# The AB layer's gaps: unread products ahead of the first weights, x by a second queue, gate rows in three pieces, an earlier reload of x

## The chip, the cores and the metric

One core of a Trainium2 chip runs the whole program. The metric is the device time of one execution in microseconds, the median over several runs. TensorE multiplies, VectorE and ScalarE work on tiles, GpSimd (POOL) does some elementwise work, and SyncE (SP) issues most transfers; ScalarE can issue transfers too. Each engine runs its own instructions strictly in order. The profile also gives the share of full clock speed that TensorE was granted.

## The reference

The program is one step of a small decoder trunk on 544 rows (a prompt of 512 and 8 samples of 4), in float32. Layer 0 is the AB mixer (four mLSTM heads and four GLA heads out of one input projection, one output projection) and an MLP; layer 1 is an SSD mixer and an MLP. After each of the four blocks comes a residual sum and a layernorm.

```
mq, mk, mv, mo, mi, mf, gq, gk, gv, gg, ga = split(x @ w_in)
ml  = headnorm(mLSTM(mq, mk, mv, gates(mi, mf))) * sigmoid(mo)
gla = headnorm(GLA(gq, gk, gv, decay(ga))) * silu(gg)
x   = LN(alpha * x + concat(ml, gla) @ w_out)
x   = LN(alpha * x + squared_relu(x @ w1) @ w2)
```

The states of both mixers, for the prompt and for the samples, are outputs as well.

## The kernel before

Activations lie with features on the 128 partitions and rows along the free axis, in two halves of 272 rows. To keep float32 accuracy each dense product is split: a weight tile `whi` + `wlo` and an activation `xh` + `xl`, and `dense` issues three products (hi hi, hi lo, lo hi) for each of eight blocks of features, so 24 for a tile and a half. `WeightStream` loads a weight tile (`wraw`, three buffers), ScalarE casts it to `whi` and VectorE subtracts to get `wlo`. `take_x` does the same with x; the gate's weight tile (the first) and the first half of x come in four pieces each, piece by piece in turn, all by SyncE's queue.

TensorE's order is the order in which the code is written. Beside the dense products run lanes: generators (`gla_lane`, `ml_lane`, `tokmajor`) that are advanced by `tick()`, which `dense` calls ahead of each product. A lane that yields a number n stays still for n products, so the table `W` spaces the small work (W["gates"] = 120 is the distance from the gates' rows to their use). `need(key)` makes a lane wait until a key is ready. The other engines' instructions are put in order by a scheduler's estimate, except where `hold()` keeps some behind named instructions.

The dense tiles of the AB layer are the gate, gq, gk, gv, mq, mk, mv, gg and mo (25 tiles in all, five at the start for one half of the rows after the other, four at the end likewise). The names that matter here:

- `head_out` makes one head's output: products `num` into two PSUM tiles, statistics on VectorE, `hf` and `hn` (the normalised head) on ScalarE with `hb` from VectorE, then, one step later, the transposes `hot` and the scaled result `cg`.
- `ml_gates` computes the gates' rows: cumulative sums and maxima on 4 partitions in the tiles `rw` and `uw`, after all GLA scores; then, 120 products later, TensorE's transposes `uwt` and eight small products `sc`.
- `ml_head` is one mLSTM head: `row_bc` copies a row to all partitions (`rowbc`), VectorE and ScalarE make the decay matrix `E` of it, GpSimd masks it, products `md`, `mo1`, `mo2` give the scores, and `head_out` ends it. `pipeline` runs the steps of several heads together; the tuple (3, 0, 1, 2) says which step of which head comes first.
- `sample` handles the eight samples' state; its 32 small products are `snum`.
- `finish` multiplies with the output gate and splits into xh and xl; then the residual of the output projection reads x again (`xf`, reloaded by `load_xf` on ScalarE's queue) when a PSUM tile of it is evacuated.

PSUM tiles for dense products are `psd` (three). All others come from `pm`:

```
k = spare[0] and turn[0] % 5 == 0
return psm.tile([P, 512], F32, tag="k" if k else "m", name=name, bufs=1 if k else 4)
```

so four calls in five rotate over four banks and each fifth call gets a fifth bank. SBUF tiles of the AB layer lie in one pool, `ab`; the pool of xf is opened when that is closed.

Of the kernel before, what the change touches and what calls it, by code (L numbers as in the profile page):

```python
# [34 lines left out]
W = dict(dec=12, gates=120, sc=16, lev=14, v=8, kd=10, out=38, ss=40, end=12, c0=20, u=13, s=16, ml=12, mr=40, dt=238, sg=72, sx=14, sq=26, so=48, l0=12, l1=12, v0=64, v1=55, f0=16, f1=18)  # L35
# [192 lines left out]
def trunk_kernel(ctx, tc, a, stages=("ab", "mlp0", "ssd", "mlp1")):  # L228
# [15 lines left out]
    S.preload_act_table_set("natural_log_exp_and_others")  # L244

# [41 lines left out]
    def take_x(pool, bufs=12):  # L287

        loaded = [None]

        def part(h, k):
            t = pool.tile([P, 2, TH], F32, tag="ft", name="xin", bufs=bufs)
            loaded[0] = nc.sync.dma_start(out=t, in_=a["xT"][h, :, k:k + 2]).ins
            split(xh[h][:, k:k + 2], xl[h][:, k:k + 2], t)
        order = {mybir.EngineType.SP, mybir.EngineType.Activation, mybir.EngineType.DVE}
        with tc.high_priority(), tc.manual_schedule(engines=order):
            ws._emit([lambda k=k: part(0, k) for k in range(0, KT, 2)])
            ws.ahead(HEAD)
            for k in range(0, KT, 2):
                part(1, k)  # L300
        nc.sync.dma_start(out=lnp, in_=a["lnp"])
        return loaded[0]
# [322 lines left out]
    def ab(pool):  # L625
# [13 lines left out]
        selr = pool.tile([P, 4, P], F32R, name="selr", bufs=1)  # L639
# [16 lines left out]
        rb = pool.tile([P, NP], F32R, name="rb", bufs=1)  # L656
# [82 lines left out]
        def head_out(mx, key, h, sT, enm=None):  # L739
# [33 lines left out]
            V.scalar_tensor_tensor(nb, mean, -1.0, f, ALU.mult, ALU.mult)  # L773
            hn = sc("hn")
            for i in range(4):
                S.activation(hn[:, i * P:(i + 1) * P], num[i][:, :128], AF.Identity, scale=f[:, i:i + 1], bias=nb[:, i:i + 1])
# [148 lines left out]
        def gla_scores():  # L925
# [7 lines left out]
            for j in range(2):  # L933
                z = pool.tile([P, NP], F32, name=f"zk{j}", bufs=1)
                G.memset(z, 0.0)
                zk.append(z)
            skz = gla["skz"] = [pool.tile([P, 2, 4, NS], F32, name=f"skz{j}", bufs=1) for j in range(2)]
# [3 lines left out]
            for q in range(2):  # L941
                sT = gla["sT"][q] = pool.tile([P, 10, 2, P], F32, tag="sT", name="sT", bufs=2)
# [12 lines left out]
                for L in LEVELS[::-1] + (128, 256):  # L955
# [12 lines left out]
                    zq = pool.tile([P, 2, 256], F32, tag="zq", name="zq", bufs=2)  # L968
# [37 lines left out]
        def hold():  # L1006

            st = ExitStack()
            for x in gla["last"]:
# [83 lines left out]
        def ml_gates():  # L1093
            rw = pool.tile([P, T], F32, name="rw", bufs=1)
            uw = pool.tile([P, T], F32, name="uw", bufs=1)
# [4 lines left out]
            yield from need("gscores")  # L1100
            with hold():
# [11 lines left out]
                V.tensor_tensor_scan(out=M, data0=M, data1=u1, initial=0.0, op0=ALU.add, op1=ALU.max)  # L1113
# [845 lines left out]
```

## Time and profile before

| | us |
|---|---|
| median of three runs (lowest to highest) | 1535.07 (1534.1 to 1536.0) |
| the profiled execution | 1528.88 |
| its span | 1527.2 |
| TensorE busy / VectorE / ScalarE / GpSimd | 1485.8 / 1091.9 / 794.9 / 235.8 |
| first product of the first layernorm (the AB mixer is over) | 288.30 |

The profile is of one execution. "Busy" of TensorE counts a product from its start to its modelled end, and products overlap, so a busy TensorE need not be at its best rate; the granted clock and the time from product to product say more. In a row of the timeline stand the start, the length, the engine, the line of the kernel, the operation, output <- inputs, shapes, and in brackets how long the engine was idle ahead of it and whom it waited for.

### The profile page before, as it was taken

The page shows a single profiled execution, that of the slowest core. Times are in us where ns is not written, and L with a number is a line of the kernel's source. Part 1 is how long each engine was busy: PE and PEld are TensorE (multiplying, and loading weights), DVE is VectorE, ACT ScalarE, POOL GpSimd, SP SyncE. Part 2 cuts the span into 40 slices and gives each one's busy share as a digit, 9 for nine tenths or more (in the row PEclk, how much of TensorE's full clock was granted, in tenths as well). Part 3 has the DMA queues.
Part 4 walks back from the last instruction along what each step waited for, and adds up shares of the span by engine and source line. Part 5 has one row for each costly group of instructions (what it writes and reads, how often), then busy time and mean ns, then how long its engine had stood idle before and what let it go on. Part 6 is the DMA issues. An engine that isn't in the chain of part 4 may idle for free.

```text
span 1527.2 us, 29115 instructions
## 1 busy us (share of the span) xinstructions
PE 1485.8 (97%) x11611; PEld 1434.4 (94%) x11611; DVE 1091.9 (72%) x2004; ACT 794.9 (52%) x1727; POOL 235.8 (15%) x298
## 2 busy tenths in 40 slices
PE   8999999999999999999999999999999999999997
PEld 7999999899999999999888788989999999999996
DVE  4974476676776677667899988777678677676656
ACT  5644447374444444536786675554347345345343
POOL 0510322010000000022454444420020000000000
PEclk9999999999999999999999999999999999999998
DMA  6321213403333232425457767364222332333221
GB/s 218 96 69 42 101 46 97 174 23 107 99 99 97 84 97 83 142 76 176 118 132 251 228 188 237 97 195 152 72 73 70 94 90 92 97 91 91 69 84 59
DMA packets 81200, 172.10 MB, mean 113 GB/s; under 512 B 9240, under 2 KB 35736, under 8 KB 80808
## 3 DMA queue, kind: packets, MB, share of 16 engines
q1 hardware_dynamic: 52248, 141.20, 29.7%
q10 hardware_dynamic: 26032, 18.29, 4.5%
q0 software_dynamic: 2784, 10.75, 1.8%
q8 instruction: 91, 1.49, 0.4%
q14 instruction: 45, 0.37, 0.1%
HBM read 153.48 MB, written 16.73 MB: 111 GB/s over the span
## 4 chain that ended last, share of the span: by engine, by line
PE 80%; DVE 10%; ACT 4%; DMA 3%; issue 2%; SPq 0%; POOL 0%; ACTq 0%; DVEq 0%
PE psd L361 53%; PE psd L504 17%; DVE wlo L167 2%; ACT whi L166 1%; PE num L749 1%; DVE acc L1442 1%; DMA h0n<-h0n 1%; PE yp L1548 1%; ACT xf L440 1%; PE gs L979 1%; PE it L1595 1%; DVE h0n L1608 1%; PE sp L1526 1%; DMA wraw<-mlp_w 1%; PE ip L1523 1%
## 5 line engine op out<-in xcount | busy, mean ns | idle before, releaser
L361 PE MATMUL psd<-xh,whi 128*128 128x272 f32 x1504 | 447.9, 298 | 9.7 <-ACT xh L283 5.0
L361 PE MATMUL psd<-xh,wlo 128*128 128x272 f32 x1504 | 444.7, 296 | 0.4 <-DVE wlo L167 0.4
L361 PE MATMUL psd<-xl,whi 128*128 128x272 f32 x1504 | 442.2, 294 | 2.5 <-DVE xl L284 2.5
L361 PEld LDWEIGHTS psd<-xh,whi 128*128 128x128 f32 x1504 | 287.1, 191 | 16.8 <-issue 7.7
L361 PE MATMUL psd<-hh,whi 128*128 128x272 f32 x1024 | 296.6, 290 | 4.1 <-DVE xf L395 3.0
L361 PEld LDWEIGHTS psd<-xl,whi 128*128 128x128 f32 x1504 | 287.4, 191 | 9.7 <-DVE xl L284 4.3
L361 PE MATMUL psd<-hh,wlo 128*128 128x272 f32 x1024 | 295.7, 289 | 0.0
L361 PE MATMUL psd<-hlo,whi 128*128 128x272 f32 x1024 | 295.4, 288 | 0.2
L361 PEld LDWEIGHTS psd<-xh,wlo 128*128 128x128 f32 x1504 | 287.0, 191 | 4.4 <-issue 2.6
L167 DVE TENSOR_TENSOR wlo<-wraw,whi 128x1024 fp32r<-128x1024 f32 (+2 forms) x173 | 208.2, 1206 | 65.3 <-ACT whi L166 63.5
L166 ACT CAST whi<-wraw 128x1024 fp32r<-128x1024 f32 (+2 forms) x173 | 174.2, 1011 | 152.3 <-PE psd L361 134.0
L361 PEld LDWEIGHTS psd<-hh,whi 128*128 128x128 f32 x1024 | 192.8, 188 | 6.3 <-DVE xf L395 4.9
L361 PEld LDWEIGHTS psd<-hlo,whi 128*128 128x128 f32 x1024 | 192.8, 188 | 0.7 <-DVE hlo L284 0.6
L361 PEld LDWEIGHTS psd<-hh,wlo 128*128 128x128 f32 x1024 | 192.8, 188 | 0.2
L395 DVE TENSOR_TENSOR xf<-xf,psd 128x272 f32<-128x272 f32 x208 | 88.4, 435 | 77.9 <-PE psd L361 77.4
L504 PE MATMUL psd<-xh,whi 128*128 128x272 f32 x416 | 120.2, 289 | 1.0 <-DVE xf L395 1.0
L504 PE MATMUL psd<-xh,wlo 128*128 128x272 f32 x416 | 119.9, 288 | 0.0
L504 PE MATMUL psd<-xl,whi 128*128 128x272 f32 x416 | 119.6, 288 | 0.0
L202 ACT CAST whi<-wsum 128x1024 fp32r<-128x1024 f32 x52 | 54.3, 1044 | 120.4 <-PE psd L504 72.0
L202 ACT CAST whi<-wraw 128x512 fp32r<-128x512 f32 (+1 forms) x52 | 43.2, 835 | 97.4 <-PE psd L361 83.8
L203 DVE TENSOR_TENSOR wlo<-wsum,whi 128x1024 fp32r<-128x1024 f32 x52 | 63.7, 1225 | 23.1 <-ACT whi L202 23.1
L504 PEld LDWEIGHTS psd<-xh,whi 128*128 128x128 f32 x416 | 78.2, 188 | 1.7 <-DVE xf L395 1.5
(475 smaller groups left out, 2824.5 us busy)
## 6 DMA issues: line engine op xcount, KB each, us to landing
wraw<-mlp_w SPq DMA_DIRECT2D x80, 512.0 KB, 3.7
wraw<-ssd_in SPq DMA_DIRECT2D x40, 512.0 KB, 4.2
wraw<-mlp_w SPq DMA_DIRECT2D x64, 256.0 KB, 3.1
wraw<-ab_in SPq DMA_DIRECT2D x24, 512.0 KB, 3.7
h<-h SPq DMA_DIRECT2D x32, 256.0 KB, 4.3
h0n<-h0n SPq DMA_DIRECT2D x16, 512.0 KB, 4.9
E<-d_cs ACTq DMA_DIRECT2D x16, 512.0 KB, 4.7
s_h<-h0n POOLq DMA_DIRECT2D x16, 512.0 KB, 4.7
```

The costliest lines, as they stand in the source:

```text
L166: nc.scalar.copy(hi[:, r], w[:, r])
L167: nc.vector.tensor_tensor(lo[:, r], w[:, r], hi[:, r].bitcast(F32), ALU.subtract)
L202: self.cut[0] = nc.scalar.copy(hi, x).ins
L203: self.cut[1] = nc.vector.tensor_tensor(lo, x, hi.bitcast(F32), ALU.subtract).ins
L361: last[0] = TE.matmul(ps[:, :TH], wt[:, k, :], rt, start=i == 0, stop=i == n - 1).ins
L395: V.tensor_tensor(x, x, ps, ALU.add)
L440: S.activation(x[:, j], x[:, j], AF.Identity, scale=g[:, j:j + 1], bias=b[:, j:j + 1])
L504: last[0] = TE.matmul(ps, wt[:, k], bt[:, k], start=first and n == 0, stop=n == 11, skip_group_check=not first).ins
L749: TE.matmul(num[i], sT[:, i] if j == i else sT[:, (4, 7, 9)[j] + i - j - 1], vt[key][:, j, h, :w], start=j == 0, stop=j == i)
L979: TE.matmul(p[:, 2 * m * b:2 * m * (b + 1)].rearrange("p (e t) -> p e t", e=2), z[:, 2 * m * b:2 * m * b + P], zq[:, :, m * b:m * (b + 1)] ...
L1442: V.scalar_tensor_tensor(acc[:, :n], ci[:, w:w + n], cw[:, m, w:w + 1], acc[:, :n], ALU.mult, ALU.add)
L1523: TE.matmul(ip[:, j * P:(j + 1) * P], hT[:, j * P:(j + 1) * P], Cf[:, tk], start=True, stop=True)
```

## The change

1. `take_x`: the four pieces of the first half of x are loaded by ScalarE's queue ahead of everything else on it; the activation table is loaded after that (it was ScalarE's first instruction).
2. `warm`, a new lane, issues products of `ones` with `ones` into a PSUM tile that nobody reads: nine ahead of the first dense product, two after each of the first three groups of six, and four more after the gate tile. It takes a turn of `pm`, so all later turns move by one.
3. `ml_gates` waits for the first, second and third GLA head in place of the end of the scores, and its three pieces are held behind the last instructions (`hb`, `hn`) of those heads. `uwt` comes 30 products after the fourth head, and `sc` in two parts, 8 products apart.
4. The order of steps in the mLSTM pipeline becomes (3, 1, 2, 0): the row copy of the newest head comes last.
5. Some tiles of the AB layer move to a second pool, `early`, on the right side of SBUF. It is closed after the first half of the last four tiles (`then()`), and the pool of xf opens there, so xf's four loads are written at that place.

```diff
-W = dict(dec=12, gates=120, sc=16, ...
+W = dict(dec=12, gates=30, gr=8, sc=16, ...
-    S.preload_act_table_set("natural_log_exp_and_others")
...
+        def load(eng, h, k):
             t = pool.tile([P, 2, TH], F32, tag="ft", name="xin", bufs=bufs)
-            loaded[0] = nc.sync.dma_start(out=t, in_=a["xT"][h, :, k:k + 2]).ins
+            return t, eng.dma_start(out=t, in_=a["xT"][h, :, k:k + 2]).ins
+
+        def cut(h, k, t):
             split(xh[h][:, k:k + 2], xl[h][:, k:k + 2], t)
...
-            ws._emit([lambda k=k: part(0, k) for k in range(0, KT, 2)])
+            ts = [load(S, 0, k)[0] for k in range(0, KT, 2)]
+            S.preload_act_table_set("natural_log_exp_and_others")
+            ws._emit([lambda k=k: cut(0, 2 * k, ts[k]) for k in range(KT // 2)])
...
+            mx["head"] = [v.ins, s.ins]
+            ready.add((key, h))
             yield
...
-            yield from need("gscores")
-            with hold():
+            yield from need(("g", 0))
+            with hold("head"):
                 S.activation(t, z, AF.Abs)
...
+            yield from need(("g", 1))
+            with hold("head"):
                 m = b
...
+            yield from need(("g", 2))
+            with hold("head"):
                 nM = uw[96:100]
...
+            yield from need(("g", 3))
             yield W["gates"]
             p = pm("uwt")
...
+            yield W["gr"]
             p = pm("sc")
...
+            yield W["gr"]
             for q in range(2):
...
-            yield from pipeline([ml_head(h) for h in range(4)], W["mr"], (3, 0, 1, 2))
+            yield from pipeline([ml_head(h) for h in range(4)], W["mr"], (3, 1, 2, 0))
...
+        def warm():
+            w = pm("warm")
+            for n, gap in ((9, 6), (2, 5), (2, 5), (2, 5), (4, None)):
+                for _ in range(n):
+                    TE.matmul(w[:, :P], ones, ones, start=True, stop=True)
+                if gap:
+                    yield gap
+
+        launch(warm(), "warm")
...
                 until("mheads")
+                then()
...
+                def take_place():
+                    early.close()
+                    xs.append(stk.enter_context(tc.tile_pool(name=f"x{n}", bufs=1, side="right", reuse_waits="tile")))
+                    new_xf(xs[0])
+                    for h in range(2):
+                        for k in range(0, KT, 4):
+                            load_xf(h, k)
```

The tiles `selr`, `rb`, `zk`, `skz`, `sT`, `zq`, `rw`, `uw` and the mLSTM heads' `E` are those that move to `early`.

What stands on SyncE's queue at the start, before and after. `wraw<-ab_gate` are the gate tile's pieces, `xin<-xT` pieces of x, `wraw<-ab_in` whole weight tiles; the counters DMAHW0 to 7 are taken in turn by all transfers in the order of the program, and a wait for one is a wait for an earlier transfer's landing. Before:

```order
L162 DMA wraw<-ab_gate 128x256
L293 DMA xin<-xT 128x544
L301 DMA lnp<-lnp 128x64
L162 DMA wraw<-ab_gate 128x256
L645 DMA prm<-ab_prm 128x13
L293 DMA xin<-xT 128x544
L162 DMA wraw<-ab_gate 128x256 [waits DMAHW0_49]
L293 DMA xin<-xT 128x544 [waits DMAHW1_49]
L165 DMA wraw<-ab_in 128x1024 [waits DMAHW2_49]
L165 DMA wraw<-ab_in 128x1024 [waits DMAHW3_49]
```

After (x's first half is on ScalarE's queue, with the counters 0, 2, 4 and 6):

```order
L162 DMA wraw<-ab_gate 128x256 x3
L302 DMA lnp<-lnp 128x64
L647 DMA prm<-ab_prm 128x13 [waits DMAHW0_49]
L162 DMA wraw<-ab_gate 128x256 [waits DMAHW1_49]
L165 DMA wraw<-ab_in 128x1024 [waits DMAHW2_49]
L165 DMA wraw<-ab_in 128x1024 [waits DMAHW3_49]
```

The last gate piece now stands behind a wait for the first piece of x, and the first whole weight tile waits for the second piece of x.

TensorE's order where the third mLSTM head's row is copied (`psd` rows are dense products). Before:

```order
L361 MATMUL psd<-xh_73,whi 128x272
L676 MATMUL rowbc<-rb,selr 128x256 x2
L1188 MATMUL md<-mq,kz 128x128 x4
L1191 MATMUL mo_2165<-mq,kz 128x384
L1194 MATMUL mo_2168<-mq,kz 128x256
L1195 MATMUL mo_2168<-mq,kz 128x128
L749 MATMUL num<-vt,E 128x130 x10
L361 MATMUL psd<-xl_75,whi 128x272
```

After:

```order
L362 MATMUL psd<-xh_72,whi 128x272
L1199 MATMUL md<-mq,kz 128x128 x4
L1202 MATMUL mo_2173<-mq,kz 128x384
L1205 MATMUL mo_2176<-mq,kz 128x256
L1206 MATMUL mo_2176<-mq,kz 128x128
L751 MATMUL num<-vt,E 128x130 x10
L678 MATMUL rowbc<-rb,selr 128x256 x2
L362 MATMUL psd<-xl_74,whi 128x272
```

The row copy went from the front of the step to its end; the rest stayed.

ScalarE's order where xf is loaded. Before, behind the casts of three weight tiles of the output projection:

```order
L283 CAST xh_74<-sy 128x4x32
L283 CAST xh_74<-cg 128x240
L166 CAST whi<-wraw 128x1024 x3
L310 DMA xf_3062<-xT 128x1088 x2
L310 DMA xf_3063<-xT 128x1088 x2
L166 CAST whi<-wraw 128x1024 x2
```

After, in the first of the last four tiles (`mo`), between the third and the last mLSTM head's normalisation (`hn`, `hf`):

```order
L778 ACTIVATE hn<-num,hb,hf 128x128 x4
L726 ACTIVATE mo<-psd 128x272
L727 ACTIVATE mo<-mo 128x272
L728 ACTIVATE mo<-mo 128x272
L730 ACTIVATE mo<-mo 128x272
L311 DMA xf_2852<-xT 128x1088 x2
L311 DMA xf_2853<-xT 128x1088 x2
L772 ACTIVATE hf<-hf,epsc 128x4
L773 ACTIVATE hf<-hf 128x4
```

The four loads moved ahead by some forty of ScalarE's instructions.

51 lines of the change are left out of this document (25 added, 26 removed).

## Prediction, made before the changed kernel ran

> **What bounds the kernel now.** I read the page's first part, then the waits of TensorE over the AB layer (0 to 420 us of the span), then its busy time and granted clock in slices of 2 us, and last the timeline around each place found.
>
> ```profile
> span 1527.2 us, 29115 instructions
> ...
> PE 1485.8 (97%) x11611; PEld 1434.4 (94%) x11611; DVE 1091.9 (72%) x2004; ACT 794.9 (52%) x1727; POOL 235.8 (15%) x298
> ```
>
> TensorE is busy for 1485.8 of 1527.2 us, so only 41 us of it are idle in the whole span, and what the change can win is idle time or slow time of TensorE. These are its waits in the AB layer (engine, what it ran, whom it waited for, us in total, times, longest):
>
> ```profile
> engine line waited for: us in total, times, longest us
> PE psd L361 <- ACT xh L283: 5.0, 1, 5.0
> PE psd L361 <- DVE xf L393: 2.8, 1, 2.8
> PE hot L780 <- ACT hn L776: 2.1, 1, 2.1
> PE num L749 <- DVE E L1175: 1.9, 1, 1.9
> ...
> ```
>
> The first product waits 5.0 us for x; 2.8 us go to the residual's reload of x (xf); 2.1 us to the normed rows of the first GLA head (hn); 1.9 us to the E of an mLSTM head. In slices (the columns are PE, PEld, DVE, ACT and POOL busy with counts, then granted clock, DMA share and GB/s):
>
> ```profile
> 120.00:122.00 2.00, 2.00 (x11) 2.00 (x11) 1.23 (x4) 0.00 (x0) 0.00 (x0) 0.50 0.42 168
> ...
> 144.00:146.00 2.00, 2.00 (x10) 2.00 (x11) 0.92 (x7) 0.56 (x2) 0.00 (x0) 0.50 0.00 0
> 146.00:148.00 2.00, 2.00 (x14) 2.00 (x13) 0.00 (x0) 0.39 (x1) 0.00 (x0) 0.74 0.00 0
> ...
> 216.00:218.00 2.00, 2.00 (x11) 2.00 (x11) 1.97 (x2) 0.00 (x0) 1.47 (x1) 0.50 0.02 4
> ...
> 270.00:272.00 2.00, 1.75 (x8) 1.78 (x9) 1.73 (x6) 0.00 (x0) 0.00 (x0) 0.50 1.02 418
> 272.00:274.00 2.00, 2.00 (x13) 2.00 (x13) 0.00 (x0) 1.05 (x1) 0.00 (x0) 0.67 1.02 413
> ```
>
> The clock is granted at 0.50 four times, each about 3.4 us long: behind the hn wait (120), behind the small products sc (144), behind the sample products snum (216), behind the xf wait (270). So an idle gap of 2 us costs its own length and, after it, up to half of a slow stretch.
>
> **The start.** DMA share and rate; the dense products (L361: busy, count, clock) before, in and after the stretch that follows 13.8 us; and the rows that set it:
>
> ```profile
> 2.00:10.00 8.00, 1.00 0.80 256
> ...
> 5.00:13.80 8.80, 7.89 (x26) 1.00 0.79 277
> 13.80:17.20 3.40, 3.38 (x15) 1.00 0.68 212
> 17.20:32.00 14.80, 14.80 (x118) 1.00 0.68 255
> ...
> 0.82 1.28 ACT L244 ACT_TABLE_LOAD   x1 [0.82 <-PEq L1949]
> 0.91 0.17 DVE L277 MEMSET ones<- 128x128 f32 x1 [0.91 <-PEq L1949]
> ...
> 9.95 0.65 ACT L283 CAST xh<-xin 128x544 fp32r<-128x544 f32 x1 [0.27 <-DMA xin<-xT]
> ...
> 11.47 1.04 ACT L166 CAST whi<-wraw 128x1024 fp32r<-128x1024 f32 x1 [0.87 <-DMA wraw<-ab_in]
> ...
> 13.82 0.59 PE L361 MATMUL psd<-xh,wlo 128*128 128x272 f32 x1 [0.44 <-DVE wlo L167]
> ```
>
> From 13.8 to 17.2 us 15 products take 3.38 us, 0.225 us each; after that 118 take 14.80, 0.125 each. The clock column reads 1.00 there, but the products say that the first 41 run at about half rate. Up to 13.82 they are paced by data: the last piece of x is cast at 9.95 on landing, the second weight tile at 11.47 on landing, and its low half releases TensorE at 13.82.
>
> The change puts nine unread products ahead of the first real one, two after each six, four after the gate tile. Such a product shows as two records; ten of the same kind (num, in the next fence) take 2.40 us at full clock and 3.90 at mostly half. Nine are 2.2 to 3.5 us from the end of the memset of ones (1.08 us), so done by 4.6, before the 5.0 of the first product: they cost nothing. The six between the groups take 0.24 to 0.39 each and stand where TensorE waits for x anyway (26 products of 0.225 are 5.9 of the 8.8 us from 5.0 to 13.8); the four ahead of the second weight tile stand in its wait. Now 3.4 us without a gap, from 13.8 on, ended the half rate; in the new order six products (1.35) and two unread ones (up to 0.78) fill the 2.0 us from one piece of x to the next (7.95 and 9.95), so the same should come before 12. What it buys is the full clock from 13.8 on: 15 x 0.100 = 1.5 us.
>
> x by ScalarE's queue: four DMA issues stand ahead of the table load (1.28 us). At 0.34 us an issue (265.90 below) the load ends near 3.5, about the time of the first cast now (3.2 by the same timeline), so it is a few tenths at most. On SyncE's queue the transfers take turns on eight counters, and a ninth waits for the first: the small prm load now waits for the first x piece, the last gate piece behind it, and the second weight tile's load for the second x piece. So weights aren't asked for earlier than now. Bytes up to the second tile are the same 2.2 MB at the same 256 GB/s; the share of 0.80 leaves room to about 1.02 (the slices at 270), 330 GB/s, which would land x 1.9 us earlier. "DMA: Bandwidth & Descriptors" of the Trainium skill (Issuing engines are not separate DMA queues) speaks against this: a second issuer saves issue time alone, so by the rule the start brings the clock's 1.5 us and by the row up to 3.4. I take 1.5, because landing (0.27 and 0.87 us of waiting), not issue, ends the waits in the rows above. Bounds: a gain of 3.4, a loss of 1.5 if x, now sharing with weights, lands late and the clock stays low.
>
> **The gates' rows.** The first GLA head's normalisation and the next two products of heads, and the same step at the second head:
>
> ```profile
> 109.29 2.40 PE L749 MATMUL num<-vt,sT 128*128 128x128 f32 x20
> ...
> 116.53 0.23 DVE L753 BATCH_NORM_AGGREGATE bmv<-bst 128x2 f32<-128x6 f32 x2
> ...
> 118.17 1.50 ACT L776 ACTIVATE hn<-num,hb,hf 128x128 f32<-128x128 f32 x4 [0.85 <-DVE hb L773]
> 118.68 1.52 PE L780 MATMUL hot<-con,hn 128*128 128x128 f32 x4 [2.11 <-ACT hn L776]
> ...
> 120.00 3.90 PE L749 MATMUL num<-vt,sT 128*128 128x128 f32 x20
> ...
> 129.08 0.60 PE L780 MATMUL hot<-con,hn 128*128 128x128 f32 x4
> 129.52 2.40 PE L749 MATMUL num<-vt,sT 128*128 128x128 f32 x20
> ...
> 138.28 2.40 PE L749 MATMUL num<-vt,sT 128*128 128x128 f32 x20
> ```
>
> The head's products end at 111.69, but its statistics are aggregated only at 116.76, since VectorE runs some 7 us of 4-row work on the gates in between; hn then starts at 118.17 and hot waits. hot to the end of num takes 118.68 to 123.90; undisturbed (129.08 to 131.92) it takes 2.84. With the 2.11 us of waiting that is 7.33 against 2.84, so 4.5 us are lost here. Now the gates come in three pieces, each behind a head's hb and hn, and behind the first head VectorE has only statistics and one weight tile's low half (1.2 us). By the durations on this path (statistics 0.7, two hf 0.5, a cast 1.0, the low half 1.2, hb 0.1, hn 1.5) hn ends near 116.8, against 116.6 when TensorE gets there: 0.2 left. The second head shares VectorE with the first piece, whose scan (1.3 us) can stand ahead of its aggregate; hn then ends about when hot comes, 0 to 1.3 us late. I take 3.7 of the 4.5 (bounds 1.0 and 4.5). The pieces' reader, uwt, now stands 31 products behind the last head's num: 140.68 + 3.9 = 144.6 on the old scale; the third piece starts behind the third head's hn, some 9 us ahead of that, and is about 4 us long. The two store DMAs of p_m and s_m move two weight loads later on SyncE's queue and only wait shorter there.
>
> sc: the eight small products go in two parts with five dense products and a transpose between. The slices at 144 and 146 were granted 0.50 and 0.74: (0.50 + 0.26) x 2 us = 1.5 us lost. I take all of it (bounds 0 and 1.5).
>
> **The mLSTM heads.** Row broadcast of head 2, mask of its E, and the two halves of num of head 1:
>
> ```profile
> 188.39 0.40 PE L676 MATMUL rowbc<-rb,selr 128*128 128x256 f32 x2
> ...
> 195.31 0.64 POOL L1180 TENSOR_SCALAR_AFFINE_SELECT E<-E 128x512 f32<-128x512 f32 x1 [0.69 <-ACT E L1179]
> ...
> 202.37 0.83 PE L749 MATMUL num<-vt,E 128*128 128x130 f32 x6
> ...
> 205.09 1.80 PE L749 MATMUL num<-vt,E 128*128 128x130 f32 x14 [1.89 <-DVE E L1175]
> ```
>
> num breaks off after three products and waits 1.89 us for VectorE's reading of rowbc. PSUM tiles rotate over four banks, each fifth going to a fifth bank: rowbc of head 3 is the 85th, the second num tile the 90th, so it waits for rowbc's slow readers. In the new order the 85th is hot, read once by VectorE, and rowbc comes last. Gain 1.7 (bounds 0 and 1.9). The price: E of the next head starts some 4.7 us of products later in its step (they end at 193.5). From rowbc at 188.39 to the mask's end at 195.95 takes 7.6 us; the next step's products begin 11.5 us later (199.9), so it still fits, with little to spare: a rival below.
>
> **The reload of x.** num of the last head, the four loads, and what waits:
>
> ```profile
> 230.20 2.40 PE L749 MATMUL num<-vt,E 128*128 128x130 f32 x20
> ...
> 265.90 0.34 ACTq L310 DMA_DIRECT2D xf<-xT  x1
> 266.27 1.62 ACTq L310 DMA_DIRECT2D xf<-xT  x3
> ...
> 269.66 1.13 DVE L393 SCALAR_TENSOR_TENSOR xf<-xf,psd 128x272 f32<-128x272 f32 x3 [0.86 <-DMA xf<-xT]
> 270.25 0.57 PE L361 MATMUL psd<-xh,whi 128*128 128x272 f32 x1 [2.80 <-DVE xf L393]
> ...
> 272.77 1.05 ACT L166 CAST whi<-wraw 128x1024 fp32r<-128x1024 f32 x1 [5.60 <-DMA wraw<-ab_out]
> ```
>
> The loads are issued from 265.90, land at 269.66, and TensorE resumes at 270.25, 2.80 us late, and then slowly: 0.50 x 1.75 us busy + 0.33 x 2.00 = 1.5 us more (the slices at 270 and 272). Now they stand on ScalarE's queue ahead of the last head's hf, and xf1 waits for that head's num (ends 232.60). So they land near 242, 20 us before their first reader. ScalarE waits for that num's statistics there anyway; four issues of 0.34 to 0.54 put hf back by at most 2 us, and hot of that head had 1.6 us to spare (hn ends 237.7, hot at 239.3). Late next would be the weight that is cast at 272.77: its tile's turn comes near 279.5, and without xf beside it it lands earlier. Gain 4.0 of the 4.3 (bounds 2.8 and 4.3).
>
> **The sum.** 1.5 + 3.7 + 1.5 + 1.7 + 4.0 = 12.4. The shifted PSUM turns and ScalarE's later hf are worth a new wait somewhere; I put 1.0 (bounds 0 and 4): 11.4 us. The profiled execution took 1528.88 us (span 1527.2 and 1.7 around it), so 1517.5 for it; the runs' median of 1535.07 lies 6.2 higher, and with that carried along I predict 1523.7. Nothing behind the AB layer is edited, and TensorE is nearly full there, so the gain is kept to the end. A change under 0.2% (3.1 us) can't be told from none here.
>
> **Rivals.**
> Half clock comes back elsewhere. The waits go, but windows fall otherwise: snum has two places in the layer and only one dropped the clock; sc may still. With the start's gain gone and two stretches of 1.5 more, 11.4 - 1.5 - 3.0 = 6.9: 1528.2. For it: the 1.9 us wait at num was followed by no slow stretch, the 2.1 us at hot was, so places lie near the edge. Against: sc's products now have dense ones between them. The Trainium skill, "TensorE: Matmul & The Clock Gate" (Part 1: The HAM clock gate), says that the rate is decided in a free-running window of about 3.4 us that doesn't reset at a kernel's start, by which the places that drop would differ from run to run; the four stretches' length agrees, and one trace can't show the phase. 0.16.
> More than said: x does land earlier (3.4) and snum keeps its clock (1.5): 14.8, 1520.3. 0.08.
> New waits eat it, the change does nothing: E late or hot late at several heads, 8.3 to 14.5 us in all; 1532 to 1538. 0.09.
> Slower: the E chain alone. If the longer queue on VectorE and POOL stretches 7.6 us by more than 4, products of E stall three steps, each with a half clock behind it. It decides where each step loses over 4.8 us ((11.4 + 3.1) / 3): 3.3 of waiting and 1.5 of slow clock; at 5.5 a step 1535.07 - 11.4 + 16.5 = 1540.2. Against: rowbc's broadcast is consumed without the products' reads in between. 0.05.
> The forecast has 0.62. So faster 0.86, same 0.09, slower 0.05. The range runs from 1517.5, the best bounds of all terms (3.4 + 4.5 + 1.5 + 1.9 + 4.3 + 1.5 = 17.1, 1518.0), to 1531, past the first rival.
>
> **What would show it.** Right: among the waits of TensorE xf, hot and num are gone or under 0.6 us each; products near 14 us take 0.125 us; no granted 0.50 near 120, 144 and 270 (minus the shift); first product still near 5.0; xf loads issued near 225 to 232. Wrong: first product after 6 us; hot waiting again behind a scan; a wait on E or on rowbc at the mLSTM heads; ScalarE idle ahead of the loads.

## The result, and the profile after

| | kernel before | changed kernel |
|---|---|---|
| median of five runs each, us (lowest to highest) | 1534.1 (1532.24 to 1536.0) | 1524.57 (1520.91 to 1527.57) |
| ratio, 95% interval | | 0.9937 (0.9918 to 0.9956) |
| profiled execution, us | 1528.88 | 1524.82 |
| first product of the first layernorm (mu) in its profile, us | 288.30 | 281.10 |

The change is faster by 9.5 us (by the interval, 6.7 to 12.6), where 1523.7 was forecast. The sum came out, but not term by term: of two terms nothing is seen (the start and `sc`), three were about right, and a wait that the prediction had not named took 2.5 us. The page of the changed kernel, span and TensorE's line:

```profile
span 1523.1 us, 29189 instructions
...
PE 1485.6 (98%) x11649; PEld 1434.2 (94%) x11649; DVE 1092.1 (72%) x2004; ACT 793.2 (52%) x1727; POOL 234.6 (15%) x298
```

Busy time is what it was (1485.8), with the unread products now in it, so by this count the span's 4.1 us between these two executions are idle time. The waits of TensorE in the AB layer (0 to 420 us), as in the prediction's second fence:

```profile
engine line waited for: us in total, times, longest us
PE vtr L696 <- ACT mv L734: 2.6, 1, 2.6
PE psd L362 <- ACT xh L281: 2.1, 2, 1.2
PE psd L362 <- DVE xl L282: 1.6, 3, 0.8
PE psd L362 <- DVE xf L396: 1.3, 1, 1.3
PE warm L1288 <- DVE ones L275: 1.1, 1, 1.1
PE var L430 <- DVE lnq L427: 0.8, 1, 0.8
```

The three waits that were to go are gone: xf (2.8), hn (2.1) and E (1.9). One is new, and longer than two of them: vtr, the transposes of an mv tile, waits 2.6 us for ScalarE's copy of it. The slices of 2 us in the AB layer in which the granted clock was under 0.9 (columns as in the prediction):

```profile
164.00:166.00 2.00, 2.00 (x14) 2.00 (x13) 0.04 (x1) 0.00 (x0) 1.96 (x2) 0.64 0.47 115
166.00:168.00 2.00, 2.00 (x10) 2.00 (x10) 1.46 (x1) 0.27 (x1) 1.41 (x1) 0.50 0.39 152
168.00:170.00 2.00, 2.00 (x11) 2.00 (x10) 1.52 (x7) 0.59 (x1) 0.48 (x1) 0.50 0.00 0
170.00:172.00 2.00, 2.00 (x10) 1.55 (x9) 0.12 (x1) 0.00 (x0) 0.14 (x1) 0.65 0.00 0
...
212.00:214.00 2.00, 2.00 (x12) 2.00 (x12) 1.34 (x2) 0.81 (x4) 2.00 (x3) 0.59 0.02 4
214.00:216.00 2.00, 2.00 (x12) 2.00 (x12) 1.61 (x4) 0.00 (x0) 1.42 (x3) 0.56 0.03 8
```

Nothing is slow near 120, 144 and 270 any more, but the first snum, which had kept its clock in the profile before, now has a stretch of double length behind it: (0.36 + 0.50 + 0.50 + 0.35) x 2 = 3.4 us lost. The start, and its stretch from 13.8 us on:

```profile
1.13 3.69 PE L1288 MATMUL warm<-ones 128*128 128x128 f32 x18 [1.13 <-DVE ones L275]
...
5.65 0.39 PE L362 MATMUL psd<-xh,whi 128*128 128x272 f32 x1 [0.82 <-ACT xh L281]
...
10.38 0.40 ACT L166 CAST whi<-wraw 128x256 fp32r<-128x256 f32 x1 [2.59 <-DMA wraw<-ab_gate]
10.69 0.64 ACT L281 CAST xh<-xin 128x544 fp32r<-128x544 f32 x1
...
11.38 0.39 PE L362 MATMUL psd<-xh,whi 128*128 128x272 f32 x1 [1.24 <-ACT xh L281]
```

```profile
13.80:17.20 3.40, 3.40 (x29) 3.35 (x28) 2.57 (x3) 1.60 (x3) 0.00 (x0) 1.00 0.69 254
```

Products run at full rate behind the fillers, the unread products (27 dense ones instead of 15 from 13.8 to 17.2; the row's 29 counts all records), but the first dense product starts at 5.65 instead of 4.99, and the last piece of x is cast at 10.69 instead of 9.95. It isn't x that is late. This is x's queue from 0 to 7.6 us (packets, MB, share of the DMA engines):

```profile
q10 hardware_dynamic: 576, 1.11, 42.9%
```

That is all of the first half of x, where in the profile before the last piece landed at 9.9. What is late is the gate's last weight piece. Its load was issued at 5.28 instead of 4.57, behind the wait for the first piece of x that "The change" shows, and ScalarE waits 2.59 us for it (the row at 10.38) before it can cast the last piece of x.

The GLA heads, and ScalarE's rows ahead of the new wait:

```profile
114.99 0.74 PE L784 MATMUL hot<-con,hn 128*128 128x128 f32 x4
115.57 2.40 PE L751 MATMUL num<-vt,sT 128*128 128x128 f32 x20
...
123.30 1.38 PE L784 MATMUL hot<-con,hn 128*128 128x128 f32 x4
124.51 2.40 PE L751 MATMUL num<-vt,sT 128*128 128x128 f32 x20
...
131.71 0.38 PE L696 MATMUL vtr<-con,mv 128*128 128x128 f32 x2
134.65 0.44 PE L696 MATMUL vtr<-con,mv 128*128 128x128 f32 x2 [2.56 <-ACT mv L734]
135.30 0.60 PE L784 MATMUL hot<-con,hn 128*128 128x128 f32 x4
```

```profile
130.99 1.50 ACT L778 ACTIVATE hn<-num,hb,hf 128x128 f32<-128x128 f32 x4
132.51 0.61 ACT L672 CAST rb<-uw 4x512 fp32r<-4x512 f32 x1
133.15 0.23 ACT L1142 ACTIVATE wi<-wi 4x32 f32<-4x32 f32 x1
133.29 1.03 ACT L166 CAST whi<-wraw 128x1024 fp32r<-128x1024 f32 x1
134.22 0.37 ACT L734 COPY mv<-psd 128x272 f32<-128x272 f32 x1
```

hot of the first head no longer waits, the second head's takes 1.38 instead of 0.60, and at the third the gates' second and third piece have made ScalarE late: the mv copy stands behind hn, the cast of rb and a weight's cast, and vtr waits for it. The mLSTM head and xf:

```profile
201.44 2.40 PE L751 MATMUL num<-vt,E 128*128 128x130 f32 x20
203.59 0.48 PE L678 MATMUL rowbc<-rb,selr 128*128 128x256 f32 x2
...
228.76 1.91 ACTq L311 DMA_DIRECT2D xf<-xT  x4
...
258.88 0.43 DVE L394 SCALAR_TENSOR_TENSOR xf<-xf,psd 128x272 f32<-128x272 f32 x1
```

num runs its 20 records in one piece, and xf is loaded 30 us ahead of its first reader.

Where the gain arose, read from the starts of the same products in both profiles. Since the chip dropped the clock at other places in other executions, a second profile of each kernel (taken as an experiment, below) stands beside it. In brackets is what slow clock took of the time, 1.7 us for each stretch of 3.4 us; the parts left out take the same in all four to 0.1 us:

| from ... to ... (us between their starts) | before | before, again | changed | changed, again |
|---|---|---|---|---|
| start to la, the first product behind the start's tiles | 31.9 | 30.3 | 30.5 | 30.3 |
| num of GLA head 0 to ss behind num of head 1 | 22.8 (1.7) | 22.4 (1.7) | 19.2 | 19.2 |
| that ss to hot of head 2 (vtr in between) | 5.7 | 5.7 | 8.2 | 8.2 |
| that hot to fst (uwt and sc in between) | 19.5 (1.7) | 18.0 | 18.4 | 20.0 (1.7) |
| fst to vstk (first snum in between) | 15.0 | 18.2 (3.4) | 18.2 (3.4) | 18.2 (3.4) |
| vstk to supd of the third mLSTM step | 51.1 (1.7) | 52.7 (3.4) | 48.8 (1.7) | 48.9 (1.7) |
| last fst of the layer to mu | 39.8 (1.7) | 39.0 (1.7) | 35.4 | 35.4 |

### The profile page after: what moved, and what is told of

Read it like the earlier page. It is cut to its first block, busy times and chain, and to the rows that moved or that the text cites. A ratio compares the mean times of both kernels' runs of the same rounds, so it can differ in the third digit from the quotient of the medians.

```text
span 1523.1 us, 29189 instructions
## 1 busy us (share of the span) xinstructions
PE 1485.6 (98%) x11649; PEld 1434.2 (94%) x11649; DVE 1092.1 (72%) x2004; ACT 793.2 (52%) x1727; POOL 234.6 (15%) x298
## 4 chain that ended last, share of the span: by engine, by line
PE 84%; DVE 7%; ACT 4%; DMA 3%; issue 1%; POOL 0%; ACTq 0%; SPq 0%; DVEq 0%; POOLq 0%
PE psd L362 56%; PE psd L505 17%; DVE wlo L167 1%; PE yp L1570 1%; PE num L751 1%; ACT whi L166 1%; PE gs L983 1%; ACT xf L441 1%; PE sp L1548 1%; PE it L1617 1%; PE ip L1545 1%; DMA E<-d_cs 1%; DVE acc L1464 1%; PE snum L848 1%; DMA h0n<-h0n 1%
## 5 line engine op out<-in xcount | busy, mean ns | idle before, releaser
L362 PEld LDWEIGHTS psd<-xh,whi 128*128 128x128 f32 x1504 | 284.4, 189 | 11.5 <-issue 5.0
```

The source lines that it names most:

```text
L362: last[0] = TE.matmul(ps[:, :TH], wt[:, k, :], rt, start=i == 0, stop=i == n - 1).ins
```

## The experiments

All ratios are to the kernel before, timed on the same chip in turn with it; an interval is 0.25 to 0.5% wide, 4 to 8 us, so most single parts (1 to 3 us) can't be told apart by time. I therefore read each profile in the same way: from la to the first mu, less what slow clock took there, which leaves work and waits alone. The changed kernel's two profiles give 245.5 and 245.4 by that measure, so it resolves some tenths of a us; the kernel before gives 249.6 and 248.1, of which the shorter wait for xf explains 1.0.

| kernel | la | mu | between | slow clock | rest | ratio (95% interval) |
|---|---|---|---|---|---|---|
| before | 31.90 | 288.30 | 256.4 | 6.8 | 249.6 | |
| before, again | 30.31 | 288.59 | 258.3 | 10.2 | 248.1 | |
| changed | 30.51 | 281.10 | 250.6 | 5.1 | 245.5 | 0.9937 (0.9918 to 0.9956) |
| changed, again | 30.28 | 282.52 | 252.2 | 6.8 | 245.4 | 0.9939 (0.9917 to 0.9961) |
| one filler | 31.50 | 283.7 | 252.2 | 6.8 | 245.4 | 0.9957 (0.9939 to 0.9975) |
| x by SyncE's queue | 31.00 | 281.6 | 250.6 | 5.1 | 245.5 | 0.996 (0.9944 to 0.9977) |
| gates in one piece | 31.23 | 282.2 | 251.0 | 6.8 | 244.2 | 0.997 (0.9953 to 0.9987) |
| old order of mLSTM steps | 31.71 | 284.9 | 253.2 | 5.1 | 248.1 | 0.9963 (0.995 to 0.9975) |
| xf's loads written late | 30.09 | 280.7 | 250.6 | 5.1 | 245.5 | 0.995 (0.9932 to 0.9967) |
| xf's place free late | 31.80 | 283.9 | 252.1 | 5.1 | 247.0 | 0.9952 (0.9937 to 0.9968) |
| vtr later | 31.74 | 279.7 | 248.0 | 5.1 | 242.9 | 0.993 (0.991 to 0.9951) |
| snum spread | 29.82 | 280.0 | 250.2 | 1.7 | 248.5 | 0.995 (0.9932 to 0.9969) |
| vtr later, more fillers | 31.16 | 277.59 | 246.4 | 3.4 | 243.0 | 0.99 (0.9875 to 0.9924) |
| that and snum spread | 31.88 | 284.0 | 252.1 | 6.8 | 245.3 | 0.9945 (0.9926 to 0.9964) |

### Both kernels a second time

No edit. Expected of the kernel before:

> The kernel before, unchanged, for a second profile of it. Theory (what differs behind the AB layer is variation from run to run): the same waits in the AB layer to 0.1 us (xh 5.0, xf 2.8, hn 2.1, E 1.9), but slow stretches at other places, and from the second sums of the first MLP's layernorm (687.9) to the first ones behind the SSD mixer (1117.5) a time that differs from the 429.6 us of its first profile by 1 us or more. Rival (the change slows the SSD mixer): 429.6 again within 0.3 us.

and of the changed one:

> The changed kernel, unchanged, for a second profile and more times. Theory: waits as in its first profile (vtr 2.6); la between 29.8 and 31.8, the first layernorm between 280 and 284 us, the SSD part 427 to 434 us in place of 433.1; ratio 0.994. Rival (its first profile is typical): SSD part 433 again, snum's slow stretch of 3.4 us at 164 to 172 again.

The kernel before took 1533.55 us in this one execution. Its waits in the AB layer:

```profile
PE psd L361 <- ACT xh L283: 5.0, 1, 5.0
PE hot L780 <- ACT hn L776: 2.1, 1, 2.1
PE num L749 <- DVE E L1175: 1.9, 1, 1.9
PE psd L361 <- DVE xf L393: 1.8, 1, 1.8
```

Three of the four are the same to 0.1 us; xf waited 1.0 less. The slow stretches are not the same: behind snum 3.4 us, near 206 (behind the E wait) 1.7, and none at sc. Rows of its start, and the slice at sc:

```profile
10.61 0.43 PE L361 MATMUL psd<-xh,wlo 128*128 128x272 f32 x1
...
11.89 0.29 PE L361 MATMUL psd<-xh,whi 128*128 128x272 f32 x1
12.01 0.29 PE L361 MATMUL psd<-xl,whi 128*128 128x272 f32 x1
```

```profile
144.00:146.00 2.00, 2.00 (x18) 2.00 (x17) 0.00 (x0) 0.00 (x0) 0.00 (x0) 1.00 0.00 0
```

Here products reach full rate by 11.9 us with no filler at all (first profile: 17.2), la comes at 30.31, and the eight small products sc cost no clock. Both terms had been read from one execution and were that execution's luck.

The changed kernel's second profile has the wait of vtr again (2.5 us), la at 30.28, the first layernorm at 282.52 and a ratio of 0.9939, all as the theory had it; the rival's signs, 433.7 us for the SSD part and the slow stretch at the first snum, are there too.

Behind the AB layer, from the second sums of the first MLP's layernorm to the first ones behind the SSD mixer, the four profiles took 429.6 (before), 433.8 (before, again), 433.1 (changed) and 433.7 us (changed, again). The ten profiles of the other experiments took 429.9 to 436.8. The order of the instructions there is the same in both kernels. So the 3.5 us by which the first two profiles differ lie within the variation from run to run: the theory held on this point, and no slowing of the SSD mixer is seen.

### One unread product in place of nineteen

```diff
-            for n, gap in ((9, 6), (2, 5), (2, 5), (2, 5), (4, None)):
+            for n, gap in ((1, 6), (0, None)):
```

> The changed kernel with one unread product at the start in place of seventeen; the turn of the PSUM tile is kept, so nothing else moves. Theory (the fillers raise the clock): products run at 0.225 us again up to about 17 us, the first product of the GLA decay (la) comes at 31.9 to 32.0 us instead of 30.5, and the time is 1.4 us longer, 1526.0, ratio to the kernel before 0.9947. Rival (x on the second queue did it, the fillers do nothing): la stays at 30.5 and the time at 1524.6.

The changed kernel has 9 + 2 + 2 + 2 + 4 = 19 of them, not the seventeen of the text above. la came at 31.50, between theory and rival, the median was 1524.98 and the ratio 0.9957. Its clock at the start:

```profile
14.00:16.00 2.00, 2.00 (x11) 2.00 (x10) 1.38 (x2) 1.44 (x2) 0.00 (x0) 0.50 0.80 197
```

Products ran at half rate to 10.0 us, at full rate from 10.6, and lost the clock again at 13.5 to 17. But the kernels with all fillers and x by ScalarE had la at 30.51, 30.28, 30.09, 31.23, 31.71, 31.80, 31.74 and 29.82, 30.9 in the mean, and three of them lost the clock at 12 to 16.5 as well. Those three have la at 31.71 to 31.80, the other five at 29.82 to 31.23. So the single 31.50 lies within their spread, and the kernel before has 31.90 and 30.31. The fillers do raise the clock early: full rate begins at 6.1 to 6.6 us in ten of the eleven profiles with all of them (10.7 in the last one below), at 11.6 with one filler and at 11.8 and 17.4 without. A gain at la isn't shown, and 0.2 us (31.1 to 30.9) is the best estimate from these means.

### x by SyncE's queue again

```diff
-            ts = [load(S, 0, k)[0] for k in range(0, KT, 2)]
...
-            ws._emit([lambda k=k: cut(0, 2 * k, ts[k]) for k in range(KT // 2)])
+            ws._emit([lambda k=k: cut(0, 2 * k, load(nc.sync, 0, 2 * k)[0]) for k in range(KT // 2)])
```

> The changed kernel with the first half of x loaded by SyncE's queue piece by piece between the gate's pieces, as before; the fillers stay. Theory (landing bounds the start, and a second issuer buys nothing): first product at 5.0 in place of 5.65 us, the fourth piece of x cast at 9.95 in place of 10.7, full rate from 7 us on, la at 30.0 to 30.6 as with the second queue, time 1524 to 1525. Rival (the second queue is worth what its text says): la 1 us or more later, 31.5, time 1525.7.

The first product started at 5.09, earlier than in any of the eleven profiles with the second queue (5.27 to 5.65). The last piece of x was cast at 10.46, la came at 31.00, between theory and rival, and mu at 281.6: these lie within the second queue's spread. The time, 1526.26 and 0.996, has an interval that overlaps the changed kernel's. So the second issuer buys nothing here that could be seen. From 2 to 12 us the core moved 271 GB/s in the changed kernel's profile, 271 in this one and 275 in the first of the kernel before; up to 10 us two issuers were ahead (293 against 241 and 256). In the eleven profiles with the second queue the last byte of x's first half was moved at 7.0 to 7.4 us; here and before, the cast of its last piece still waited for it at 10.46 and 9.95. But a group of products needs its weights too, and the gate's last piece came behind x, so the earlier x brought nothing that could be seen. The Trainium skill, "DMA: Bandwidth & Descriptors" (Issuing engines are not separate DMA queues), says that issuing from several engines saves issue time alone; over 2 to 12 us the trace agrees (271 and 271 GB/s).

### The gates' rows in one piece

```diff
-W = dict(dec=12, gates=30, gr=8, ...
+W = dict(dec=12, gates=120, gr=0, ...
-            yield from need(("g", 0))
-            with hold("head"):
+            yield from need("gscores")
+            with hold():
...
-            yield from need(("g", 1))
-            with hold("head"):
+            with hold():
... (the waits for ("g", 2), ("g", 3) and both yields of gr go likewise)
```

> The changed kernel with the gates' rows in one piece behind the GLA scores, uwt 120 products later and sc in one part, as before. Theory (the parts add up): hot of the first GLA head waits 2.1 us for hn again and loses 4.5 us with the slow clock behind it; on the other side the 0.8 us at the second head and the new 2.6 us wait of vtr for mv go, and sc loses 1.2 us again. Net 4.5 - 0.8 - 2.5 + 1.2 = 2.4 us longer, 1527.0, ratio 0.9953. Rival (vtr's wait is not the gates' doing but comes from the earlier start): vtr still waits 2.6 us, net 4.9 longer, 1529.5, ratio 0.997.

```profile
PE hot L784 <- ACT hn L778: 2.1, 1, 2.1
```

hot waits 2.1 us again with a slow stretch behind it, and the wait of vtr is gone from the list: it is the gates' doing, so the rival falls. But the net was over-estimated. From num of head 0 to ss behind head 1 it lost 3.3 us (22.6 against 19.2), won 2.5 at vtr (5.7 against 8.2) and won 0.4 at sc (18.0 against 18.4): 0.4 us between la and mu, not 2.4. Without the slow stretch behind hot it would even be 1.3 faster (244.2 against 245.5). The time, 1526.96 and 0.997, does not decide between 0.4 and 2.4: beside it on the same chip xf's loads written late, which is in effect the changed kernel again (below), has 0.995, 3 us less, with overlapping intervals. So the three pieces by themselves moved a wait from hot to vtr.

### The old order of the mLSTM steps

```diff
-            yield from pipeline([ml_head(h) for h in range(4)], W["mr"], (3, 1, 2, 0))
+            yield from pipeline([ml_head(h) for h in range(4)], W["mr"], (3, 0, 1, 2))
```

> The changed kernel with the old order of steps (3, 0, 1, 2) in the mLSTM pipeline. By the turns of the PSUM tiles the 75th is then rowbc and the 80th the second num tile of one step, which get the same bank. Theory (bank turns make the wait): num waits 1 to 2 us for VectorE's reading of rowbc near 191 us, one step earlier than in the kernel before: 1.9 us longer, 1526.5, ratio 0.995; 3.4 if a slow stretch follows. Rival (the wait came of VectorE being late with E altogether): the wait is at the same step as before, near 202 us, with the same length. Second rival: the shift by one turn was enough, no wait, 1524.6.

```profile
189.07 0.40 PE L678 MATMUL rowbc<-rb,selr 128*128 128x256 f32 x2
191.50 0.83 PE L751 MATMUL num<-vt,E 128*128 128x130 f32 x6
194.81 1.80 PE L751 MATMUL num<-vt,E 128*128 128x130 f32 x14 [2.47 <-DVE E L1186]
```

num breaks off after three products and waits 2.47 us, one step earlier than in the kernel before, where the count of PSUM turns puts it. Both rivals fall: VectorE is not late in general (the wait moved with the turns by one step), and the shift alone isn't enough. The rest from la to mu is 2.6 us longer (248.1 against 245.5), the median 1525.6. The bank turns make this wait: shown.

### xf's loads written late, and xf's place free late

First the loads alone at their old place in the code, with the second pool kept:

```diff
-                    ab(pool, early.enter_context(...), take_place)
+                    ab(pool, early.enter_context(...), lambda: None)
...
+                take_place()
                 xp = xs[0]
```

> The changed kernel with the four loads of xf written where they stood before, behind the AB layer's pool; the second pool of tiles stays. Theory: issued when the last tiles have been read, near 258 us, they land late again, the dense products wait 2.8 us for xf and lose 1.5 us more to a slow stretch: 4.4 us longer, 1529.0, ratio 0.9966. Rival (the later weight tiles now arrive earlier and hide it, or the SSD stage gives the gain back anyway): under 1.5 us longer at the end, though the first layernorm starts 4.4 us later.

```profile
228.39 1.91 ACTq L311 DMA_DIRECT2D xf<-xT  x4
```

The loads were issued where the changed kernel issues them (228.76), no wait for xf came back, and mu was at 280.7. Theory and rival both fall: ScalarE's order is set by the scheduler, and it puts the loads as early as the memory under xf is free. In effect this is a further run of the changed kernel. Then all tiles in one pool again:

```diff
-                    ab(pool, early.enter_context(tc.tile_pool(name="abr", ...)), take_place)
+                    ab(pool, pool, lambda: None)
...
+                take_place()
                 xp = xs[0]
```

> The changed kernel with all tiles of the AB layer in one pool again and the pool of xf opened when that is closed, so that xf's place comes free only with the whole layer (writing the loads later alone had changed nothing: they were still issued near 228 us). Theory: the loads are issued near 258 us on the new scale, the dense products wait 2.8 us for xf, and a slow stretch may follow (1.5 us): the first layernorm starts 2.8 to 4.4 us later, 283.5 to 285.5 where the last tiles start at the same time, and the time is 1528.5, ratio 0.997. Rival: the weights' loads beside it take the blame, no wait for xf over 1 us, time as for the changed kernel, 1524.6.

```profile
262.40 0.82 ACTq L311 DMA_DIRECT2D xf<-xT  x2
...
267.24 0.37 PE L362 MATMUL psd<-xh,whi 128*128 128x272 f32 x1 [1.27 <-DVE xf L394]
```

Now they are late, and TensorE waits. So the place in memory, not the line in the code, is what the change bought here. The wait is 1.27 us, though, against 2.80 and 1.8 in the two profiles before, and no slow stretch followed: 1.5 us (247.0 against 245.5), between theory and rival. In both kernels the loads stand behind the casts of the same three weight tiles; here they were issued 0.2 us behind the start of the first of these casts, in the first profile before 1.7 us. Why the three waits differ is left open.

### vtr later

```diff
-            yield W["v"]
+            yield W["v"] + (28 if key == "m" and h < 3 else 0)
             p = pm("vtr")
```

> The changed kernel with the transposes of the first three mv tiles (vtr) 28 dense products, 3.5 us, later. Theory (the new wait is a queue: mv's copy on ScalarE stands behind hn of the third head, rb's cast and a weight's cast): the copy is done 2.5 us after vtr's old turn, so the wait of 2.6 us is gone, with no slow stretch near 135: 2.5 to 3.0 us less, 1521.8, ratio 0.992. Rival (ScalarE itself is behind there): another wait of TensorE of over 1.5 us takes its place between 130 and 145 us, no gain.

No wait of vtr is left, and none over 1.3 us has taken its place in the AB layer. The rest fell by 2.6 us to 242.9, as the theory had it. The median was 1520.78 and the ratio 0.993, which can't be told from the changed kernel's 0.9937. A slow stretch stands behind sc now (from 146.2 us), though sc comes in two parts here. That the wait was a queue on ScalarE is shown by this and by the rows of ScalarE above, without idle time from hn to the mv copy.

### snum spread

snum is 16 products (each shows as two records), so the edit makes four groups of four; the text below counts the records.

```diff
                     TE.matmul(nv[:, 2 * q:2 * q + 2, LS * b:LS * b + LS], c0[q][:, b], ...
+                    if b % 4 == 3 and not (q == 1 and b == NB - 1):
+                        yield 4
```

> The changed kernel with the 32 small products snum of each sample step in eight groups of four, four dense products between two groups. Theory (a window that small products fill counts as idle and halves the clock): no slow stretch at 164 to 176 and 206 to 220 us, which cost 5.1 us in the changed kernel's profile and 3.4 to 5.1 in those of four variants: 4.2 us less, 1520.4, ratio 0.991. Rival (it was the lane behind it, or half dense products is not enough): slow stretches stay, or a wait for a PSUM turn comes instead, 1524 to 1527.

```profile
164.00:166.00 2.00, 2.00 (x20) 2.00 (x19) 0.98 (x1) 0.00 (x1) 1.48 (x2) 1.00 0.03 12
166.00:168.00 2.00, 2.00 (x20) 2.00 (x18) 0.00 (x0) 0.59 (x1) 1.40 (x1) 1.00 0.75 242
```

Both stretches at snum are gone in this profile (slow clock 1.7 us in all, and that behind vtr), but the rest grew by 3.0 us, to 248.5: small waits of svar and md, and longer steps of the mLSTM heads, whose work now meets the later sample step. The median, 1526.05, shows no gain. In this profile the theory was right on the clock; on the time it was wrong.

### Two kernels with both ideas

vtr later, and eight more fillers ahead of the last piece of x:

```diff
-            for n, gap in ((9, 6), (2, 5), (2, 5), (2, 5), (4, None)):
+            for n, gap in ((9, 6), (2, 5), (2, 5), (10, 5), (4, None)):
```

> The changed kernel with vtr 28 products later (as in vtr_later) and eight more unread products ahead of the fourth piece of x, where TensorE had idled for 1.4 us. Theory: the wait of vtr is gone (2.6 us) and the clock isn't lost at 12 to 18 us any more (1.7 us in about half of the profiles): la at 30.0 to 30.6, the first layernorm near 277.5 to 279, 1521.0, ratio 0.9915. Rival (the fillers stand in x's way): la at 31.5 or later, 1522.5 or more.

1518.71 us, ratio 0.99 (0.9875 to 0.9924), against 0.9939 (0.9917 to 0.9961) for the changed kernel beside it, with intervals that just overlap: the fastest of all, 6 us by the ratios where 2.6 of waiting and some slow clock were expected. la at 31.16 is no earlier (the fillers ended 1.0 us behind the last piece of x), but the clock wasn't lost at 12 to 18. The second kernel added the spread snum, begun 12 products earlier, and two more PSUM turns at the start:

> As fixed_vtr, and the 16 products snum of each sample step in four groups of four with four dense products between them, begun 12 products earlier so that the steps behind keep their place, and two PSUM turns more at the start, by which no row broadcast shares the fifth bank with products of the same step. Theory: the slow stretches at 162 to 176 and 206 to 220 us are gone (3.4 to 5.1 us in the profiles with snum in one piece) and no new wait takes their place: first layernorm at 274 to 276 us, 1517.5, ratio 0.9895. Rival (the waits of md and svar that spreading brought come again): two stretches less but 2 us or more of new waits, 1520 to 1522.

```profile
PE snum L845 <- ACT hn L778: 1.7, 1, 1.7
```

```profile
208.00:210.00 2.00, 2.00 (x14) 2.00 (x13) 0.15 (x1) 1.75 (x4) 1.03 (x2) 0.61 0.00 0
...
216.00:218.00 2.00, 2.00 (x11) 2.00 (x10) 1.05 (x2) 0.28 (x1) 1.17 (x1) 0.50 0.04 12
```

The rival came: begun earlier, snum waits 1.7 us for the PSUM tile that a head's hn reads, and behind that idle time the clock stays at half for 10 us (5.1 us lost), although dense products stand between the groups. A stretch behind sc (from 147.0 us) came as well. 1526.11, no better than the changed kernel.

## Why the prediction was right, and where it was not

The forecast was a gain of 11.4 us, the medians give 9.5 (6.7 to 12.6), and the profiles show 7.0 in the AB layer (mean of mu in both profiles before, 288.4; in those of the changed kernel and its equal, xf's loads written late, 281.4). So the direction, the place and most of the mechanisms held, and the sum was some 4 us too high for the layer. The 2.5 us between 7.0 and 9.5 lie behind it, where nothing is edited and the SSD part alone varies by 7 us, or in the interval: the second timing gives 9.4 us, and that of its equal 7.7. That stays open. Term by term:

- **The start, 1.5: not shown.** The step that failed read the half rate of one execution as the kernel's. la spreads from 30.3 to 31.9 without fillers and from 29.8 to 31.8 with them. The prediction took it that the second queue lands x no earlier, and had set the other case at 1.9 us. x did land earlier, by some 2.5 us (7.4 against 9.9), but the gate's last weight piece came later, and that was not in the text. The four issues took 1.86 us instead of four times 0.34, so the table load ended at 4.00 and not near 3.5; with 0.65 us of waiting for the first weight piece that made the first product 0.7 later, where a few tenths were allowed.
- **Gates' rows, 3.7: measured 3.1 to 3.6** for hot of the heads 0 and 1, with 4.5 gained at the first and 0.9 lost at the second in the first pair of profiles, as the text had it (0 to 1.3).
- **sc, 1.5: nothing.** Again one execution's stretch. Without slow clock the part from hot to fst takes 17.8 and 18.0 with sc in one piece, 18.4 and 18.3 in two; and two of the eleven profiles with two pieces have a slow stretch behind them (vtr later, and the last kernel).
- **mLSTM, 1.7: 2.2** without slow clock (49.4 against 47.1 and 49.3 against 47.2 from vstk to supd), and the old order brought 2.6 back. The bank turns were the cause. The price feared for E, 7.6 us in 11.5, did not come.
- **xf, 4.0: 3.6 and 4.4** in the two pairs of profiles. Undoing it cost 1.5, since that run had a shorter wait and no slow stretch.
- **Unknown new waits, 1.0: 2.5,** one wait, vtr. The prediction listed as late next only hot of the second head and the weights; it looked at VectorE's work behind each head, and not at what ScalarE's queue holds behind the gates' pieces.

Of the 7.0, 0.8 lie ahead of la, where a gain isn't shown, and 6.2 from la to mu. There 3.4 + 2.2 + 4.0 - 2.5 - 0.4 make 6.7; slow clock at other places took 0.6 more than before, which leaves 6.1. So luck had a part in the total: two terms of 3.0 in all brought nothing that could be seen and a wait cost 1.5 more than was put down for it, but the medians gained 2.5 more than the layer did. Of what would show the prediction right, xf, hot and num are gone from the waits, xf is loaded at 228.76 (225 to 232) and no 0.50 stands near 120, 144 and 270; the first product came at 5.65, not 5.0. The rival "half clock comes back elsewhere" did happen in part: behind the first snum in both profiles of the changed kernel. But in the second profile of the kernel before it stands there too, and in the changed kernel's equal it does not, so it can't be put down to the change. Before lost 6.8 and 10.2 us to slow clock between la and mu, the changed kernel and its equal 5.1, 6.8 and 5.1: fewer waits, fewer stretches, 2.8 in the mean. The slower rival, E late at three heads, did not occur: no wait for E is left.

## What to carry to other kernels

Waits of TensorE for other engines' work came back to 0.1 us in nearly every run (hot 2.1, vtr 2.5 to 2.6); waits that hang on a transfer (x at the start, xf) did not, nor did the places where the clock drops. Take a second profile before you put a price on a slow stretch, and compare parts by work and waits with slow clock taken out. When work is moved on one engine, read the queues of the others that work with it: here a quarter of the gain went to a copy on ScalarE that stood behind the moved rows. Here the scheduler started a transfer when its memory was free (228.4 us with the loads written late, 262.4 with their place free late), so it was the pool that had to change and not the line. And when one of two inputs gets a queue of its own, look at when the other one lands.

## What the runs showed of the hardware

The clock dropped to 0.50 for 3.4 us, or two or three times that, with 1.7 us lost in each 3.4, at places that change from run to run: behind an idle gap of 2.1 us in all three profiles that had it (hot), behind one of 2.5 us (vtr) in four of eight, behind one of 1.9 or 2.5 us (E) in one of three, behind 2.8 and 1.8 us (xf) but not behind 1.3, behind sc in one of three with sc in one piece and in two of eleven with two. The Trainium skill, "TensorE: Matmul & The Clock Gate" (Part 1: The HAM clock gate), states a free-running window of about 3.4 us; the length and the variation agree with it.

A TensorE that is busy by the profile can lose its clock too. snum's 16 products of eight columns fill 3.6 us and had slow clock at their end or right behind at one or both places in each of the twelve profiles that had them in one piece. With snum spread it was gone in one profile and came in the other, behind a wait of 1.7 us, so that the small products are the cause is likely but not shown. At the start the clock column reads 1.00 while products take 0.225 us instead of 0.125; there the time from product to product is the better witness.
